# A two-layer attention and mLSTM network on one core: both value units moved behind the first pair's six projections, norm-weighted tokens on ScalarE, copies to natural order on GpSimd's queue

## The chip, the cores and the metric

The kernel runs on one core of a Trainium2 chip. The metric is the device time of one execution in microseconds (us); lower is better. Engines are named as in the profile: PE is TensorE (matmuls; PEld its weight loads), DVE is VectorE, ACT is ScalarE, POOL is GpSimd, and SP is SyncE, which issues most transfers.

## The reference

A sequence of 512 tokens of width 1024 goes through a layer of dilated attention, a feed-forward layer, an mLSTM layer and another feed-forward layer, each behind an RMS norm and with a residual, all in fp32. Only the attention layer bears on the change:

```python
def dilated_attention_mixer(xn, positions, w_in, w_out):
    proj = (xn @ w_in).reshape(B, S, N_GROUPS, 3, ATTN_HEADS, ATTN_HEAD_DIM)
    for g, (window, dilation) in enumerate(DIL_CONFIGS):          # 3 groups
        q = apply_partial_rope(proj[:, :, g, 0], positions) * scale
        k = apply_partial_rope(proj[:, :, g, 1], positions)
        v = proj[:, :, g, 2]
        o, lse = dilated_window_attention(q, k, v, window, dilation)
        ...
    wts = jax.nn.softmax(jnp.stack(lses), axis=0)
    o = jnp.einsum('gbsh,gbshd->bshd', wts.astype(xn.dtype), jnp.stack(outs))
    return o.reshape(B, S, ATTN_WIDTH) @ w_out
```

with `xn = rms_norm(x, g)`, that is x times the inverse root of its mean square per token, times a gain g per column. There are 8 heads of 128 and 3 groups, so `w_in` is 1024 x 9216.

## The kernel before, in words

**Products.** Each fp32 matrix is split into a high and a low part (`_h`, `_l`), and a product is three matmuls (high x high, high x low, low x high). Weights come in chunks of 512 KB: a load on SP's queue into one of three `wraw` buffers, then `split_chunk` (L204), in which ScalarE copies the high part (L209) and VectorE subtracts it from the chunk to get the low part (L210). There are three buffers for the high parts and three for the low ones, so the loads run a little ahead of PE. `project` (L245) makes q or k of one group for two heads: two chunks, 48 matmuls at L240 of 128x512, into two PSUM banks (suffix `_0`, `_1`), each of which VectorE evacuates (L887 or L889) and whose first 32 rows are then rotated (L521 to L527).

**Names.** `a0g1q_k0_h` is the high part of chunk 0 of the weights of attention pair 0, group 1, q. A pair is two heads; four pairs make the layer. `xa_h`, `xa_l` are the transposed tokens, already times the gain. The inverse norm (`inverse_rms`, L308) is not applied to the tokens: it is worked out beside the first projection in small instructions on 128x4 (L193, L194, L496, and others), spread over the partitions by eight diagonal matrices `xdg` (L324) and two matmuls `xbc` (L330), copied to `xrbc` (L331), and multiplied in at each evacuation.

**Order.** The program is written for the most part in the order of its work. The framework puts instructions into one queue per engine in the order in which they are written; `defer(n, f)` writes f after n more calls of `advance`, which stands after each chunk's matmuls, and `fenced` keeps other work out of a group of matmuls. An engine works through its queue strictly in order, and buffers of a pool tag (`pt`, `qk`, `v12`, `heads`, each with one or more buffers) are handed on from one tile to the next, which waits for the last reader of the one before.

**Values.** The values of group 0 (`v0`, 1024 columns) and of groups 1 and 2 (`v12`, 512 columns each, for the first two pairs) are not projected chunk by chunk. The class `Values` (L585) makes each as a 2 x 2 block product with seven block products instead of eight. This needs sums of blocks of the weights and sums of blocks of the tokens:

- The weights: `begin` (L608) loads block a11 into `first`, a21 into `own`, both on SP, and adds a22 to `own` by an accumulating transfer on GpSimd's queue (L604). `prepare` (L621) splits one chunk of the next block each time it is called, adds `first` to `own` on VectorE (L637) and adds a21 to `first` by another accumulating transfer.
- The tokens: `token_forms` (L550) scales all eight token tiles by the gain (`scaled`, L557, into `xg`), makes differences and sums of half tokens (`vz`, L567 and others) and splits four of them (T1 to T4, L538). It is written in three parts, `forms[0..2]`.
- `run` (L642) does the products in `V_ORDER`, 24 matmuls at L663 for each block product. Results of `v0` are staged in `vstage0`, `vstage1` and copied by `settle` (L693) to natural order in `v0`: 32 transfers of 64 KB, each 32x512, which may start when a stage's quarter is complete.

**The first pair before the change** goes: a0g0k and a0g0q (the first of them in an order of its own at the start of the program), then `forms[0]`, a0g1q, `forms[1]`, a0g1k, `forms[2]`, then `values_stage` (v0, then v12), then a0g2q, a0g2k. The scores of group 0 (`scores0`) are deferred by two chunks after a0g1k. While v0 runs, it calls `v12.prepare`; while v12 runs, it prefetches chunks of a0g2q.

Of the kernel before, what the change touches and what calls it, by code (L numbers as in the profile page):

```python
# [34 lines left out]
RUN_AT = (2, 2, 4, 9)  # L35
# [5 lines left out]
HALF = SEQ // 2  # L41
# [30 lines left out]
def tile_hybrid_dilated_attn_mlstm(  # L72
# [35 lines left out]
            nc.tensor.matmul(idle_ps, ones_r, idle_w, start=True, stop=True)  # L108
    idle(10)
    cols = cp.tile([P, 80], F32, name="cols")  # L110
    rows = cp.tile([80 - KC, P], F32, name="rows")
    row_of = {"attn": 0}

    def load_rows():
        r0 = KC
        for key, src in (
            ("mlstm", mlstm_norm[0:1]), ("ffn", ffn_norm), ("head", mlstm_head_gain[0:1]),
            ("convb", mlstm_conv_b[0:1]), ("convw", mlstm_conv_w[0]),
        ):
            flat = src.rearrange("a (r p) -> (a r) p", p=P)  # L120
            n = flat.shape[0]
            row_of[key] = r0
            nc.gpsimd.dma_start(rows[r0 - KC:r0 - KC + n, :], flat)
            r0 += n

    def transpose_rows():
        tp = ps.tile([P, 512], F32, tag="t", name="rowsT", bufs=1)
        nc.tensor.transpose(tp[:, :80 - KC], rows, ident[:80 - KC, :80 - KC])
        nc.vector.tensor_copy(cols[:, KC:], tp[:, :80 - KC])

    def col(key, i):
        return cols[:, row_of[key] + i:row_of[key] + i + 1]
# [7 lines left out]
    def defer(n, fn):  # L140
        later.append((tick[0] + n, next(order), fn))
# [62 lines left out]
    def split_chunk(chunk):  # L204

        raw, n, view, name = chunk
        hi = wp.tile([P, 1024], F32R, tag="whi", name=name + "_h", bufs=W_BUFS)
        lo = wp.tile([P, 1024], F32R, tag="wlo", name=name + "_l", bufs=W_BUFS)
        nc.scalar.activation(hi[:, :n], raw[:, :n], AF.Copy)  # L209
        nc.vector.tensor_tensor(lo[:, :n], raw[:, :n], hi[:, :n].bitcast(F32), op=ALU.subtract)  # L210
        return view(hi), view(lo)
# [134 lines left out]
    with ExitStack() as actx:  # L346
# [6 lines left out]
        part = lambda at, w: acst[:, at - K_MA:at - K_MA + w]  # L353
        mask_band, mask_causal, mask_dil, perm = part(K_MA, 2 * P), part(K_M1, P), part(K_M2, P), part(K_G, P)
        boot = ap.tile([P, 4, SEQ], F32, tag="v12", name="boot", bufs=2)
        cosn, sinn = boot[:R, 1], boot[:R, 2]
# [35 lines left out]
        def tok_tile(name):  # L392
            return ap.tile([P, 2, SEQ], F32, tag="qk", name=name, bufs=6)
# [12 lines left out]
        load_rows()  # L406
# [48 lines left out]

        def squares(hf):
            for tb in range(TB):
                nc.scalar.activation(boot[:, 3], xtok[:, tb, hf * 512:(hf + 1) * 512], AF.Square,
                                     accum_out=ss2[:, hf, tb:tb + 1])

        ACT, DVE = mybir.EngineType.Activation, mybir.EngineType.DVE
# [38 lines left out]
        behind(box["finish"], engine=DVE)  # L500
        for k in range(4, 8):
            x_keep(k)
        defer(5, transpose_rows)

# [45 lines left out]
        def token_forms():  # L550
            xg = ap.tile([P, KC, SEQ], F32, tag="heads", name="xg")
            lo_, hi_ = xg[:, :4], xg[:, 4:]
            z = ap.tile([P, 4, HALF], F32, tag="pt", name="vz", bufs=2)

            def scaled(ks):
                for k in ks:
                    nc.vector.tensor_scalar(xg[:, k], h[k], col("attn", k), None, op0=ALU.mult)  # L557
# [27 lines left out]
        class Values:  # L585
# [20 lines left out]
                    nc.sync.dma_start(view, self.source(key, ch))  # L606

            def begin(self):  # L608
                flat = lambda t: t.rearrange("p a s -> p (a s)")
                for key, tag in (("first", "qk"), ("own", "pt")):  # L610
                    for ch in range(2):
                        n = "%s%s%d" % (self.name, key, ch)
                        self.raw[key, ch] = (flat(tok_tile(n)) if tag == "qk" else
                                             ap.tile([P, 1024], F32, tag="pt", name=n, bufs=2))
                for ch in range(2):
                    self.load("a11", ch, self.raw["first", ch])
                for ch in range(2):
                    self.load("a21", ch, self.raw["own", ch])
                    self.load("a22", ch, self.raw["own", ch], True)
# [70 lines left out]
        def staged_values():  # L690
            stage = [ap.tile([P, TB, 512], F32, tag="v12", name="vstage%d" % i, bufs=2) for i in range(2)]

            def settle(i, c):  # L693
                for b in range(TB):
                    nc.sync.dma_start(v_all[0][32 * c:32 * c + 32, b, i * 512:(i + 1) * 512],
                                      stage[i][32 * b:32 * b + 32, c])
            return stage, settle

# [12 lines left out]
        def values_stage():  # L711
            v0_unit.prepare(2)
            v_all.append(ap.tile([P, TB, D], F32, tag="heads", name="v0"))
            v0_unit.run(v12_unit.prepare, settle)
            vq = [ap.tile([P, TB, 512], F32, tag="v12", name="vq%d" % i, bufs=2) for i in range(2)]
            v_all.append(vq[::-1])

            def g2q(n):
                ready.append(split_chunk(weight_chunk(w_in, len(ready), 6 * D, 4, "a0g2q_k%d" % len(ready))))
            v12_unit.run(g2q)  # L720

        def o_head(k):
            return v_all[0][:, :, k * P:(k + 1) * P]
# [1 line left out]
        def attention_pair(pr):  # L725
# [150 lines left out]
            for g in range(3):  # L876
# [3 lines left out]
                for part in range(2):  # L880
# [22 lines left out]
                        sh0 = sh  # L903
                    else:
                        rotate(t, sh, g == 0)
                    if pr == 0 and g == 1:
                        forms[1 + part]()
                    qk.append(t)
                if pr == 0 and g == 0:
                    forms[0]()  # L910
                if pr == 0 and g == 1:
                    values_stage()
                if g == (pr == 0):
                    defer(RUN_AT[0], lambda: run(lambda: scores0(*qks[0])))
# [757 lines left out]
```

## Time and profile before

| what | value |
|---|---|
| time, three runs | 1448.89, 1452.92, 1446.08 us, median 1448.89 |
| the profiled execution | 1448.05 us; its span 1446.2 us, mean granted clock 0.993 |
| PE busy | 1419.0 us, 98% of the span, 7968 matmuls |
| PEld busy | 1240.4 us, 86% |
| DVE busy | 991.3 us, 69% |
| ACT busy | 616.5 us, 43% |
| POOL busy | 62.7 us, 4% |
| transfers | 156.54 MB, mean 108 GB/s |

The profile is of one execution. Its span runs from the first to the last instruction and leaves out 1.85 us of what the execution's time holds around it. A row of a timeline reads: start, duration, engine, line, operation, output <- inputs, shapes and types, number of instructions joined in the row, and in brackets the idle time before it and what ended that. A row of the waits reads: who waited <- for whom, total us, how often, the longest. In rows of one engine equal instructions in a row are joined, so a row's duration can be that of several. SPq and POOLq are rows of queued transfers. Buffer numbers are left out of names, and k0 and k1 may read as `k`.

PE is busy 98% of the span, but a busy PE is not always at full pace: `PEclk` is the granted clock, and a matmul of 512 columns takes longer when it is low. So both the gaps and the slow stretches count.

### The profile page before, as it was taken

Reading aid. Unit: us, or ns where it says so; the run is one execution under the profiler, and the core shown is the slowest. Engines: PE = TensorE matmul, PEld = TensorE weight load, DVE = VectorE, ACT = ScalarE, POOL = GpSimd, SP = SyncE. Lnnn points to the kernel's source line nnn. Section 1 sums busy time; section 2 is a strip of 40 time slices with the busy share of each in tenths; the row PEclk is TensorE's granted clock in tenths of the full one; section 3 lists DMA queues with packets and bytes.
Section 4 is the critical chain, followed back from the end, with each engine's and each line's share of the span. In section 5 each row is a group of like instructions: output and inputs, shape, how many; then the busy total and the mean of one; then the engine's idle time right before and its main releaser. Section 6 shows DMA issues by size and latency. Waiting matters only on the chain. (4 is left out here: it accounts for less than half of the span.)

```text
span 1446.2 us, 20245 instructions
## 1 busy us (share of the span) xinstructions
PE 1419.0 (98%) x7968; PEld 1240.4 (86%) x7968; DVE 991.3 (69%) x1705; ACT 616.5 (43%) x1019; POOL 62.7 (4%) x99
## 2 busy tenths in 40 slices
PE   9798999999999999999999999999999999999998
PEld 7687888888888888999998888798888899998886
DVE  7865587775767487877782358987758777776233
ACT  6144432323225244444562243785534345455223
POOL 1010001010100100000000000000000000001001
PEclk9899999999999999999999999999999999999999
DMA  6465326262622534233223332221133333224231
GB/s 200 120 167 125 116 74 185 85 197 74 197 86 75 182 102 146 66 110 118 88 83 107 95 97 73 74 88 59 61 105 97 116 118 101 80 84 132 73 105 70
DMA packets 130390, 156.54 MB, mean 108 GB/s; under 512 B 6836, under 2 KB 112628, under 8 KB 130296
## 3 DMA queue, kind: packets, MB, share of 16 engines
q1 hardware_dynamic: 122928, 133.65, 29.9%
q0 software_dynamic: 5712, 20.49, 5.4%
q8 instruction: 62, 1.02, 0.3%
q10 hardware_dynamic: 1656, 1.12, 0.2%
q14 instruction: 32, 0.26, 0.1%
HBM read 143.18 MB, written 9.96 MB: 106 GB/s over the span
## 5 line engine op out<-in xcount | busy, mean ns | idle before, releaser
L1607 PE MATMUL fin<-fw_h,f1hh 128*128 128x512 f32 (+1 forms) x198 | 72.8, 368 | 0.0
L1607 PE MATMUL fin<-fw_l,f1hh 128*128 128x512 f32 (+1 forms) x198 | 72.5, 366 | 0.0
L1607 PE MATMUL fin<-fw_h,f1hl 128*128 128x512 f32 (+1 forms) x198 | 72.4, 366 | 0.0
L210 DVE TENSOR_TENSOR fw_l<-fw_w,fw_h 128x1024 fp32r<-128x1024 f32 x22 | 27.1, 1234 | 65.5 <-ACT fw_h L209 65.5
L210 DVE TENSOR_TENSOR fo_k_l<-fo_k_w,fo_k_h 128x1024 fp32r<-128x1024 f32 (+1 forms) x24 | 27.2, 1135 | 62.0 <-ACT fo_k_h L209 62.0
L240 PE MATMUL fo<-f0hh,fo_k_h 128*128 128x512 f32 x176 | 68.5, 389 | 0.0
L240 PE MATMUL fo<-f0hl,fo_k_h 128*128 128x512 f32 x176 | 68.5, 389 | 0.0
L240 PE MATMUL fo<-f0hh,fo_k_l 128*128 128x512 f32 x176 | 68.5, 389 | 0.0
L209 ACT ACTIVATE fo_k_h<-fo_k_w 128x1024 fp32r<-128x1024 f32 (+1 forms) x24 | 23.8, 990 | 74.4 <-PE fo L240 72.1
L209 ACT ACTIVATE fw_h<-fw_w 128x1024 fp32r<-128x1024 f32 x22 | 23.3, 1060 | 67.8 <-PE fin L1607 67.8
L1607 PEld LDWEIGHTS fin<-fw_l,f1hh 128*128 128x128 f32 x198 | 37.4, 189 | 6.1 <-DVE fw_l L210 0.2
L1607 PEld LDWEIGHTS fin<-fw_h,f1hl 128*128 128x128 f32 x198 | 37.3, 189 | 6.0
L1607 PEld LDWEIGHTS fin<-fw_h,f1hh 128*128 128x128 f32 x198 | 37.4, 189 | 6.0
L240 PEld LDWEIGHTS fo<-f0hh,fo_k_h 128*128 128x128 f32 x176 | 33.0, 188 | 6.9
L240 PEld LDWEIGHTS fo<-f0hl,fo_k_h 128*128 128x128 f32 x176 | 33.0, 188 | 6.8
L240 PEld LDWEIGHTS fo<-f0hh,fo_k_l 128*128 128x128 f32 x176 | 33.0, 188 | 6.8
L240 PE MATMUL f0j<-n_h,f0j_h 128*128 128x512 f32 x96 | 37.5, 390 | 0.0
L240 PE MATMUL f1j<-n_h,f1j_h 128*128 128x512 f32 x96 | 37.5, 390 | 0.0
L240 PE MATMUL f0j<-n_h,f0j_l 128*128 128x512 f32 x96 | 37.4, 389 | 0.0
L240 PE MATMUL f1j<-n_h,f1j_l 128*128 128x512 f32 x96 | 37.4, 389 | 0.0
L240 PE MATMUL f0j<-n_l,f0j_h 128*128 128x512 f32 x96 | 37.3, 389 | 0.0
L240 PE MATMUL f1j<-n_l,f1j_h 128*128 128x512 f32 x96 | 37.3, 389 | 0.0
(2132 smaller groups left out, 4892.6 us busy)
## 6 DMA issues: line engine op xcount, KB each, us to landing
f0j_w<-in_ffn_w_in_dram SPq DMA_DIRECT2D x28, 512.0 KB, 4.9
f1j_w<-in_ffn_w_in_dram SPq DMA_DIRECT2D x28, 512.0 KB, 3.6
fw_w<-in_ffn_w_out_dram SPq DMA_DIRECT2D x22, 512.0 KB, 3.8
fo_k_w<-in_ffn_w_out_dram SPq DMA_DIRECT2D x20, 512.0 KB, 3.4
awo_k_w<-in_attn_w_out_dram SPq DMA_DIRECT2D x8, 512.0 KB, 3.8
mv_k_w<-in_mlstm_w_in_dram SPq DMA_DIRECT2D x8, 512.0 KB, 3.6
mqk_k_w<-in_mlstm_w_in_dram SPq DMA_DIRECT2D x8, 512.0 KB, 3.7
mo_k_w<-in_mlstm_w_in_dram SPq DMA_DIRECT2D x8, 512.0 KB, 3.6
```

What stands on the lines that cost most here:

```text
L209: nc.scalar.activation(hi[:, :n], raw[:, :n], AF.Copy)
L210: nc.vector.tensor_tensor(lo[:, :n], raw[:, :n], hi[:, :n].bitcast(F32), op=ALU.subtract)
L240: nc.tensor.matmul(acc, whl[a][:, k, m * P:(m + 1) * P], pairs[b][kk], start=(kk == 0 and (a, b) == SPLITS[0]), stop=(kk == nk - 1 and (a, ...
L1607: nc.tensor.matmul(acc[i][:, cs], a[a_][kk][:, tb * P:(tb + 1) * P], whl[b_][:, k, cs], start=(kk == 0 and (a_, b_) == SPLITS[0]), stop=(k ...
```

## The change

Six edits, all in the attention layer's first pair or ahead of it.

1. `values_stage` stands after all six projections of pair 0 (behind a0g2k) and no longer after the first four. The three parts of the token forms stand behind a0g1k, a0g2q and a0g2k, and no longer behind a0g0q, a0g1q and a0g1k. `scores0` of group 0 is deferred by one chunk after a0g2k. Since pair 0 has no projection left, the last weights fetched while v12 runs are a1g0q's.
2. `scaled` runs on ScalarE (`activation` with a scale) and no longer on VectorE. `vz` lies in the first half of the tile `boot`; the other users of `boot` (cosines, sines, squares) move up to make room.
3. `first` and `own` of a chunk are the two halves of one tile of tag `pt` (`v0w0`, `v0w1`, `v12w0`, `v12w1`); before, `first` had tag `qk` and `own` had `pt`.
4. The 32 copies of `settle` are issued on GpSimd's queue and no longer on SP's.
5. `rows`, 72 rows of gains and biases for later layers, lies in the attention's pool (tag `ex2`) and is handed to `load_rows` and `transpose_rows`.
6. The two tiles of `v12`'s results stand in their natural order, not reversed.

```diff
-            z = ap.tile([P, 4, HALF], F32, tag="pt", name="vz", bufs=2)
+            z = boot[:, 0:2].rearrange("p a s -> p (a s)").rearrange("p (k n) -> p k n", k=4)
...
-                    nc.vector.tensor_scalar(xg[:, k], h[k], col("attn", k), None, op0=ALU.mult)
+                    nc.scalar.activation(xg[:, k], h[k], AF.Copy, scale=col("attn", k))
...
-                flat = lambda t: t.rearrange("p a s -> p (a s)")
-                for key, tag in (("first", "qk"), ("own", "pt")):
-                    for ch in range(2):
-                        n = "%s%s%d" % (self.name, key, ch)
-                        self.raw[key, ch] = (flat(tok_tile(n)) if tag == "qk" else
-                                             ap.tile([P, 1024], F32, tag="pt", name=n, bufs=2))
+                for ch in range(2):
+                    t = ap.tile([P, 2, 1024], F32, tag="pt", name="%sw%d" % (self.name, ch), bufs=2)
+                    self.raw["first", ch], self.raw["own", ch] = t[:, 0], t[:, 1]
...
-                    nc.sync.dma_start(v_all[0][32 * c:32 * c + 32, b, i * 512:(i + 1) * 512],
+                    nc.gpsimd.dma_start(v_all[0][32 * c:32 * c + 32, b, i * 512:(i + 1) * 512],
...
-            v_all.append(vq[::-1])
-
-            def g2q(n):
-                ready.append(split_chunk(weight_chunk(w_in, len(ready), 6 * D, 4, "a0g2q_k%d" % len(ready))))
-            v12_unit.run(g2q)
+            v_all.append(vq)
+
+            def following(n):
+                ready.append(split_chunk(weight_chunk(w_in, len(ready), 256, 4, "a1g0q_k%d" % len(ready))))
+            v12_unit.run(following)
...
-                    if pr == 0 and g == 1:
-                        forms[1 + part]()
                     qk.append(t)
-                if pr == 0 and g == 0:
-                    forms[0]()
-                if pr == 0 and g == 1:
+                    if pr == 0 and 3 <= 2 * g + part:
+                        forms[2 * g + part - 3]()
+                if pr == 0 and g == 2:
                     values_stage()
-                if g == (pr == 0):
-                    defer(RUN_AT[0], lambda: run(lambda: scores0(*qks[0])))
+                if g == (2 if pr == 0 else 0):
+                    defer(1 if pr == 0 else RUN_AT[0], lambda: run(lambda: scores0(*qks[0])))
```

The changed kernel's line numbers are one to five lower than those of the kernel before.

VectorE's queue around the inverse norm, before. `xr` is the norm in the making, `xg` the scaled tokens, `xrhl` its split.

```order
L193 TENSOR_TENSOR xr_a_323<-xr_a_323,xv_306 128x4
L567 TENSOR_TENSOR xg_362<-xg_362,vz_363 128x4x256
L194 SCALAR_TENSOR_TENSOR xr_320<-xr_a_323,xr_320 128x4
L572 TENSOR_TENSOR xg_362<-xg_362 128x4x256
L318 CAST xrhl_335<-xr_320 128x4
L706 TENSOR_SCALAR nrtok_354<-xr_320 128x4
L210 TENSOR_TENSOR a0g1q_k0_l_359<-a0g1q_k0_w_356,a0g1q_k0_h_358 128x1024
L319 TENSOR_TENSOR xrhl_335<-xr_320,xrhl_335 128x4
L324 TENSOR_SCALAR xdg_338<-cst_67,xrhl_335 128x128 x4
L324 TENSOR_SCALAR xdg_343<-cst_67,xrhl_335 128x128 x4
```

The same place now:

```order
L192 TENSOR_TENSOR xr_a_323<-xr_a_323,xv_306 128x4
L193 SCALAR_TENSOR_TENSOR xr_320<-xr_a_323,xr_320 128x4
L317 CAST xrhl_335<-xr_320 128x4
L703 TENSOR_SCALAR nrtok_354<-xr_320 128x4
L209 TENSOR_TENSOR a0g1q_k0_l_359<-a0g1q_k0_w_356,a0g1q_k0_h_358 128x1024
L318 TENSOR_TENSOR xrhl_335<-xr_320,xrhl_335 128x4
L323 TENSOR_SCALAR xdg_338<-cst_67,xrhl_335 128x128 x4
L323 TENSOR_SCALAR xdg_343<-cst_67,xrhl_335 128x128 x4
L209 TENSOR_TENSOR a0g1q_k1_l_475<-a0g1q_k1_w_472,a0g1q_k1_h_474 128x1024
```

The instructions on `xg` of 128x4x256 no longer stand between the small ones of the norm.

PE's queue at the first chunk of a0g1k, before:

```order
L240 MATMUL a0g1q_1_456<-xa_h3_140,a0g1q_k1_l_484 128x512
L240 MATMUL a0g1k_0_528<-xa_h0_134,a0g1k_k0_h_532 128x512
L240 MATMUL a0g1k_0_528<-xa_l0_135,a0g1k_k0_h_532 128x512
L240 MATMUL a0g1k_1_529<-xa_h0_134,a0g1k_k0_h_532 128x512
L240 MATMUL a0g1k_1_529<-xa_l0_135,a0g1k_k0_h_532 128x512
L240 MATMUL a0g1k_0_528<-xa_h0_134,a0g1k_k0_l_533 128x512
```

And now, where `rowsT` is the transpose of `rows` and a0g2q is the projection that follows:

```order
L239 MATMUL a0g1q_1_447<-xa_h3_140,a0g1q_k1_l_475 128x512
L239 MATMUL a0g1k_0_510<-xa_h0_134,a0g1k_k0_h_514 128x512
L239 MATMUL a0g1k_0_510<-xa_l0_135,a0g1k_k0_h_514 128x512
L127 MATMUL rowsT_542<-cst_67,rows_128 128x72
L239 MATMUL a0g1k_1_511<-xa_h0_134,a0g1k_k0_h_514 128x512
L239 MATMUL a0g1k_1_511<-xa_l0_135,a0g1k_k0_h_514 128x512
L239 MATMUL a0g2q_0_591<-xa_h0_134,a0g2q_k0_h_595 128x512
L239 MATMUL a0g2q_0_591<-xa_l0_135,a0g2q_k0_h_595 128x512
L239 MATMUL a0g1k_0_510<-xa_h0_134,a0g1k_k0_l_515 128x512
```

Three more instructions than before now stand ahead of the first matmul on the low part of `a0g1k_k0`: `rowsT` and two of a0g2q.

SP's queue around the copies, before:

```order
L606 DMA v12first0_874<-in_attn_w_in_dram 128x2x512
L606 DMA v12first1_875<-in_attn_w_in_dram 128x2x512
L695 DMA v0_625<-vstage0_352 32x512 x8
L695 DMA v0_625<-vstage1_353 32x512 x16
L606 DMA v12a121_w_948<-in_attn_w_in_dram 128x2x512
L606 DMA v12a220_w_1114<-in_attn_w_in_dram 128x2x512
```

The same copies now, on GpSimd's queue:

```order
L604 DMA v0w1_747<-in_attn_w_in_dram 128x2x512
L692 DMA v0_762<-vstage0_352 32x512 x15
L692 DMA v0_762<-vstage1_353 32x512 x8
L604 DMA v12w0_1011<-in_attn_w_in_dram 128x2x512
L604 DMA v12w1_1012<-in_attn_w_in_dram 128x2x512
L692 DMA v0_762<-vstage1_353 32x512 x8
L604 DMA v12w0_1011<-in_attn_w_in_dram 128x2x512
L604 DMA v12w1_1012<-in_attn_w_in_dram 128x2x512
```

SP's queue now holds loads only. On GpSimd's queue the accumulating loads of v12 (L604) stand behind copies.

PE's matmuls are the same in number and kind, and PE's order is the same again from the first chunk of the projection a1g0k to the end.

More of the change, by code (lines that the diff above doesn't have):

```diff
@@ L110, in tile_hybrid_dilated_attn_mlstm, with load_rows @@
     cols = cp.tile([P, 80], F32, name="cols")
-    rows = cp.tile([80 - KC, P], F32, name="rows")
     row_of = {"attn": 0}
-    def load_rows():
+    def load_rows(rows):
         r0 = KC
@@ L124, in load_rows, with transpose_rows @@
             r0 += n
-    def transpose_rows():
+    def transpose_rows(rows):
         tp = ps.tile([P, 512], F32, tag="t", name="rowsT", bufs=1)
@@ L355, in tile_hybrid_dilated_attn_mlstm @@
         boot = ap.tile([P, 4, SEQ], F32, tag="v12", name="boot", bufs=2)
-        cosn, sinn = boot[:R, 1], boot[:R, 2]
+        cosn, sinn = boot[:R, 2], boot[:R, 3]
         sinr = ap.tile([R, SEQ], F32, name="sinr")
@@ L405, in tile_hybrid_dilated_attn_mlstm @@
         nc.sync.dma_start(cst[:, K_MT:], consts[:, K_MT:K_MA])
-        load_rows()
+        rows = ap.tile([80 - KC, P], F32, tag="ex2", name="rows")
+        load_rows(rows)
         pair = x_tiles("xa")
@@ L457, in squares @@
             for tb in range(TB):
-                nc.scalar.activation(boot[:, 3], xtok[:, tb, hf * 512:(hf + 1) * 512], AF.Square,
+                nc.scalar.activation(boot[:, 1], xtok[:, tb, hf * 512:(hf + 1) * 512], AF.Square,
                                      accum_out=ss2[:, hf, tb:tb + 1])
@@ L502, in tile_hybrid_dilated_attn_mlstm @@
             x_keep(k)
-        defer(5, transpose_rows)
+        defer(5, lambda: transpose_rows(rows))
         def by_block(t):
```

## The prediction

> **What bounds the kernel now.** I read the windows first, to see where TensorE is not busy or not at full clock. Columns after the window and its length: busy time of PE, PEld, DVE, ACT, POOL with counts, then granted clock, DMA share, GB/s.
>
> ```profile
> 36.00:72.00 36.00, 28.60 (x105) 22.39 (x106) 32.10 (x56) 6.30 (x7) 1.19 (x1) 0.85 0.44 121
> 108.00:145.00 37.00, 33.23 (x139) 26.45 (x138) 19.16 (x17) 18.50 (x22) 2.42 (x2) 0.95 0.52 125
> 181.00:217.00 36.00, 36.00 (x178) 30.38 (x177) 29.31 (x91) 12.35 (x40) 0.00 (x0) 1.00 0.24 74
> ```
>
> In the first two PE is idle 7.4 and 3.8 us, with its clock down to 0.85 and 0.95; in the third, when the first pair is done, neither. Next the waits of PE up to 400 us: four of 2.4 us or more, all before 127 us.
>
> ```profile
> PE v_acc L663 <- ACT v12a_h L209: 3.6, 1, 3.6
> PE v_acc L663 <- DVE v0a_l L210: 3.3, 1, 3.3
> PE a0g1q L240 <- DVE rot L521: 2.9, 1, 2.9
> PE a0g1q L240 <- DVE a0g1q_k_l L210: 2.4, 1, 2.4
> ```
>
> The timeline of PE gives what each really costs (start, duration, instruction).
>
> ```profile
> 23.31 0.39 PE L240 MATMUL a0g0k<-xa_h,a0g0k_k_h 128*128 128x512 f32 x1
> 34.19 0.39 PE L240 MATMUL a0g1q<-xa_h,a0g1q_k_h 128*128 128x512 f32 x1
> 38.27 0.63 PE L240 MATMUL a0g1q<-xa_h,a0g1q_k_l 128*128 128x512 f32 x1
> 38.70 0.63 PE L330 MATMUL xbc<-xdg,ones_r 128*128 128x512 f32 x1
> 41.15 0.40 PE L240 MATMUL a0g1q<-xa_l,a0g1q_k_h 128*128 128x512 f32 x1
> 44.37 0.23 PE L128 MATMUL rowsT<-cst,rows 72*128 72x72 f32 x1
> 51.42 0.39 PE L240 MATMUL a0g1q<-xa_l,a0g1q_k_h 128*128 128x512 f32 x1
> 65.72 0.62 PE L663 MATMUL v_acc<-v0a_h,xa_h 128*128 128x512 f32 x2
> 75.29 0.39 PE L663 MATMUL v_acc<-v0a_h,xa_h 128*128 128x512 f32 x1
> 105.29 0.47 PE L663 MATMUL v_o<-v0a_h,vT4h 128*128 128x512 f32 x1 [0.42 <-DVE vstage L650]
> 118.78 0.39 PE L663 MATMUL v_acc<-v12a_h,xa_l 128*128 128x512 f32 x1
> 126.59 0.39 PE L663 MATMUL v_acc<-v12a_h,xa_l 128*128 128x512 f32 x1
> ```
>
> From 23.31 to 34.19 there are 48 matmuls, 0.2267 each. After a stall they come every 0.43 us (38.27 to 38.70) for some microseconds: the clock is paid on top of the gap. Lost, as elapsed time less instructions times 0.2267: 34.19 to 41.15, 12 of them, 4.24; 44.37 to 51.42, 11, 4.56; 65.72 to 75.29, 15, 6.17; 118.78 to 126.59, 9, 5.77. **Sum 20.74 us**; this is all that the change can win. The gap of 0.42 at 105.29 left no slow matmuls behind it.
>
> Why each stall? The first three are VectorE's. In 36:72 it is busy 32.10 of 36 us, and it got there with a late start, since the token forms stand inside the chain of small instructions that makes the inverse norm:
>
> ```profile
> 25.82 0.16 DVE L496 TENSOR_TENSOR xv<-x_ss 128x4 f32<-128x4 f32 x1 [2.49 <-ACT boot L458]
> 35.76 0.16 DVE L318 CAST xrhl<-xr 128x4 fp32r<-128x4 f32 x1
> 37.11 1.66 DVE L324 TENSOR_SCALAR xdg<-cst,xrhl 128x128 fp32r<-128x128 f32 x8
> 40.64 0.69 DVE L331 COPY xrbc<-xbc 128x512 f32<-128x512 f32 x1 [0.75 <-PE xbc L330]
> 42.45 1.20 DVE L547 SCALAR_TENSOR_TENSOR vT<-xg,vT 128x1024 fp32r<-128x1024 f32 x1
> 43.58 0.67 DVE L887 TENSOR_TENSOR a0g_q<-a0g0q,xrbc 128x512 f32<-128x512 f32 x1
> 48.46 2.33 DVE L524 TENSOR_TENSOR rot<-rot,sinr 32x1024 f32<-32x1024 f32 x2
> 50.72 1.28 DVE L527 TENSOR_TENSOR a0g_q<-a0g_q,rot 32x512 f32<-32x512 f32 x2
> 53.13 0.67 DVE L889 TENSOR_TENSOR a0g_q<-a0g1q,xrbc 128x512 f32<-128x512 f32 x1
> ```
>
> The fourth is SP's: 24 copies to natural order held its queue, and the chunk v12a121 came behind them.
>
> ```profile
> 99.71 17.89 SPq L695 DMA_DIRECT2D v<-vstage  x24
> 117.64 14.66 SPq L606 DMA_DIRECT2D v12a_w<-in_attn_w_in_dram  x3
> ```
>
> ```profile
> 121.67 1.06 ACT L209 ACTIVATE v12a_h<-v12a_w 128x1024 fp32r<-128x1024 f32 x1 [4.54 <-DMA v12a_w<-in_attn_w_in_dram]
> ```
>
> **The change part by part.** PE's matmuls are the same in number, and PE's order is the same again from the projection a1g0k on, so the sum is the stalls that go less the stalls that come.
>
> *The inverse norm comes earlier.* Without token forms between them, thirteen dependent steps of four columns run from L496 to L318. Two such rows of a later norm show the step:
>
> ```profile
> 525.54 0.16 DVE L193 TENSOR_TENSOR n1r_a<-n1r_a,n1v 128x4 f32<-128x4 f32 x1
> 525.74 0.16 DVE L194 SCALAR_TENSOR_TENSOR n1r<-n1r_a,n1r 128x4 f32<-128x4 f32 x1
> ```
>
> 13 x 0.2 is 2.6, so L318 starts at 28.4 and not 35.76. From L318 to the end of the eight xdg it was 37.11 + 1.57 - 35.76 = 2.92 (the eight overlap what follows by some 0.09); so now 31.34. In the new order the first xbc is PE's 32nd instruction from 23.31, due at 30.34; its four xdg are there about 0.8 before 31.34. Wait 0.28. It was at 38.70. Stall 1 goes: a0g1q_k0_l stands two small instructions behind L318 and takes 1.13, so it is ready by 29.9; PE wants it at 34.9.
>
> *VectorE's way to a0g1k.* Every 1024-column instruction takes 1.13 (48.46 to 50.72, two). From 31.34: a0g1q_k1_l 1.13; three readers of xbc 1.81 (40.64 to 42.45); the difference z 1.13; evacuation and rotation of both a0g0 halves 9.55 (43.58 to 53.13, the same sixteen); two evacuations of a0g1q 2.44 (a pair L887, L521 is 1.22: 43.58 to 48.46, four); a0g1k_k0_l 1.13. End 48.53. PE reaches a0g1k, 98 instructions after 23.31 and the wait, at 45.81. Five instructions later, 46.95, it wants the bank of a0g1q_1, free at 47.40: wait 0.45. After two matmuls, 47.85, it wants a0g1k_k0_l: wait 0.68. Stall 2 was for the bank of a0g0k_0: now wanted at 39.7, evacuated at 31.34 + 1.13 + 1.81 + 1.13 + 3 x 1.22 = 39.07. Gone, with 0.6 to spare.
>
> Stall 3 was for v0a110's low part, the first of the value weights. Between a0g1k_k0_l and it VectorE now has sixteen 1024-column instructions (1.13) and four evacuations with rotation (1.22 each), 23.0 us: 48.53 + 23.0 = 71.5. PE reaches it 243 matmuls after 23.31 and the waits above: 23.31 + 55.09 + 1.41 = 79.8. Stall 3 goes, with 8 us to spare.
>
> *Scaled tokens on ScalarE.* Eight of 128x512, at the price of the nearest row, 0.6:
>
> ```profile
> 12.64 2.43 ACT L227 ACTIVATE xa_h<-xT,cols 128x512 fp32r<-128x512 f32 x4 [2.01 <-PE xT L306]
> 26.15 1.07 ACT L209 ACTIVATE a0g1q_k_h<-a0g1q_k_w 128x1024 fp32r<-128x1024 f32 x1
> ```
>
> That is 4.8 us on an engine that was busy 6.30 of the 36 us from 36 on. Three stand ahead of a0g1q_k1_h: 27.1 + 1.8 + 1.0 = 29.9, wanted by VectorE at 31.34. The fourth is done by 30.6, z wants it at 34.3. Cost nothing; with that slack of 1.4 us gone, its excess would go straight into a0g1q.
>
> *Copies on GpSimd's queue.* SP no longer holds them: v12a121 follows the release of its buffer (v0a220's split, before 102) and is landed long before ScalarE can use it. Stall 4 goes. But on POOL's queue sixteen copies of the first stage and eight of the second now stand ahead of the accumulating loads of v12's own, which v12s1 needs. Rows for both:
>
> ```profile
> 104.40 1.41 DVE L650 SCALAR_TENSOR_TENSOR vstage<-v_o,nrtok,vstage 128x512 f32<-128x512 f32 x2
> 217.10 2.25 POOL L848 DMA_DIRECT2D a0pD<-a0pB  x4 [86.75 <-DVE a0pB L845]
> v12own<-in_attn_w_in_dram POOLq DMA_DIRECT2D x2, 512.0 KB, 9.9
> DMA to landing us min/median/max: 6.9/8.3/11.4
> ```
>
> In the old times: the second stage's fold frees the copies at 105.1; eight at 0.56 end at 109.6; the first load lands 9.9 later at 119.5, split on ScalarE 1.06 and VectorE 1.13: 121.7. PE, without stall 4, wants the high part at 118.78 + 13 x 0.2267 = 121.73 and the low part 0.23 later. Just in time: 0. Bounds: landing in 6.9 leaves 3 us to spare; landing in 11.4 costs 1.3 (121.7 + 1.5 - 121.96), and copies at 0.75, as SP issued them (17.89 / 24), 1.5 more, with a slow clock behind.
>
> What else moves costs nothing: v12's loads wait for v0's weights in the same buffers, as v12first did; the scores of group 0 now stand one chunk into a1g0q, whose matmuls hide their reductions; rows, boot and the order of vq change addresses only. The wait at 105.29 and its like stay.
>
> **Sum.** 20.74 - 0.28 - 0.45 - 0.68 = 19.3. Against the profiled execution, 1448.05: 1428.7. The median of the runs is 0.84 above it, so **1429.6**.
>
> On the clock: gaps of 0.42 leave none, gaps of 2.37 do. The Trainium skill (TensorE: Matmul & The Clock Gate, Why this matters for your kernels) advises against gaps over about 3 us only; the trace differs, the two gaps of 2.4 and 2.9 halved the pace. By the page they would have cost 3.4 us less and the sum would be 15.9, an estimate; the rows decide.
>
> **The rivals.** *VectorE stays late (A).* If two 1024-column instructions more come before a0g1k_k0_l, the 0.68 becomes 2.9, and the clock drops as in stall 2 (4.56 - 2.9 = 1.7): 4.0 more, 1433.6. For: VectorE works without a pause from 25.8 to 55. Against: the sum above has every instruction.
>
> *v12's adds land late (B).* 1.3 to 2.8 of stall, and of clock what stalls 1 and 4 had, 4.24 - 2.4 = 1.8 and 5.77 - 3.6 = 2.2: 1432.7 to 1434.6. For: the copies' own transfers are in flight with it. Against: this tile's four loads had a median of 8.3, and with it nothing waits.
>
> *Early loads crowd (C).* v0's weights, 1.5 MB, are loaded right behind a0g0k, and their adds run beside a0g1q_k0, which has 1.4 us to spare. If it comes 1.5 to 3 late: 0.1 to 1.6, and 1.8 of clock, 1431.5 to 1433. For: the loads stand ahead of a0g1q's on SP's queue. Against: a0g1q_k0_h was already split at 26.15, 8 us before PE wanted it.
>
> *The stalls return (D).* The change takes only the scaled tokens off VectorE:
>
> ```profile
> 25.93 0.49 DVE L557 TENSOR_SCALAR xg<-h,cols 128x512 f32<-128x512 f32 x1
> ```
>
> Eight are 3.9 us. If its waits only move, that and stall 4 are won, or stall 4 alone: 1448.89 - 9.7 = 1439.2 to 1443.1. Against: the new order puts 44 matmuls of a0g2 between VectorE's late work and its next need.
>
> *Slower: copies starve behind VectorE (E).* If each copy's descriptors had to wait out a VectorE instruction of 1.23, it would cost 0.56 + 1.23 = 1.79; sixteen from 99.71 end at 128.4, plus 11.4 to land and 2.2 to split is 142.0, 20 us after PE wants it, and 2.2 of clock: 1451.9. It is slower by over 0.5% from 1456.1, another 4.2 / 16, so from 2.05 us a copy. The Trainium skill (SBUF — State Buffer, SBUF: two separate sides) has this trap: GpSimd cannot write descriptors while VectorE holds the shared port in a two-port mode, and it advises the SP or ACT queue. Against: the four issues at 217.10 took 0.56 each beside a busy VectorE.
>
> **How the numbers follow.** Forecast 0.60, A 0.15, B 0.10, C 0.04, D 0.07, E 0.04. A measurement of this kernel can tell about 0.5%, 7.2 us. Faster by more: the first four and 0.01 of D, 0.90; within: 0.06 of D and 0.01 of E, 0.07; slower: 0.03 of E. Range: no new stall at all, 1428.2, less 2 for the runs' spread, 1426; A and B together, 1429.6 + 4.0 + 5.0, 1438.6, so 1439. It leaves out D and E, 0.11, and what I don't see.
>
> **What would show it.** Right: xbc near 30.5 us, no PE wait over 1 us before 127, granted clock 1.0 from 36 to 145, the projection a1g0k begun about 19 us earlier than before. A shows as a wait for a0g1k_k_l over 2 us; B as ScalarE waiting for v12w's DMA before v12s; C as a wait for xdg over 1 us; E as POOL issues of over 1 us. Wrong altogether if PE's lost time before a1g0k stays above 12 us.

## The result, and the profile after

The changed kernel takes 1437.79 us (median of five runs, 1434.03 to 1440.11) against 1448.89 before: a ratio of 0.9922, 95% interval 0.9892 to 0.9951. That is 11.1 us faster where 19.3 were forecast. The profiled execution took 1437.79 with a span of 1435.7; its forecast was 1428.7, so 9.1 us are missing.

The windows come first again (columns as before). The stretch from 36 to 72 is at full clock and nearly gapless; the one from 108 to 145 is not.

```profile
36.00:72.00 36.00, 35.20 (x155) 28.49 (x154) 35.60 (x54) 9.58 (x10) 0.00 (x0) 1.00 0.40 102
108.00:145.00 37.00, 33.77 (x140) 26.89 (x139) 20.59 (x20) 17.42 (x21) 16.75 (x28) 0.95 0.87 192
```

The waits of PE in the first 400 us: all four old stalls are gone. The small waits are the forecast ones; the two for `v12s` are the chunk of v12's third product.

```profile
PE v_s L660 <- ACT v12s_h L208: 2.0, 1, 2.0
PE v_s L660 <- DVE v12s_l L209: 0.8, 1, 0.8
PE a0g2q L239 <- DVE rot L521: 0.5, 1, 0.5
PE a0g1k L239 <- DVE a0g1k_k_l L209: 0.3, 1, 0.3
PE xbc L329 <- DVE xdg L323: 0.3, 1, 0.3
```

On PE's timeline that stall is seen to cost more than its 2.8 us of gaps: matmuls behind it come in twos of 1.05 and not of 0.62.

```profile
129.93 0.39 PE L660 MATMUL v_acc<-v12a_h,xa_l 128*128 128x512 f32 x1
132.37 0.49 PE L660 MATMUL v_s<-v12s_h,vT 128*128 128x512 f32 x1 [2.05 <-ACT v12s_h L208]
133.63 0.80 PE L660 MATMUL v_s<-v12s_l,vT 128*128 128x512 f32 x1 [0.77 <-DVE v12s_l L209]
134.22 1.05 PE L660 MATMUL v_s<-v12s_h,vT 128*128 128x512 f32 x2
140.57 0.39 PE L660 MATMUL v_o<-v12s_h,vT 128*128 128x512 f32 x1
180.57 0.48 PE L239 MATMUL a1g0k<-xa_h,a1g0k_k_h 128*128 128x512 f32 x1
```

From 129.93 to 140.57 stand 25 matmuls: 10.64 - 25 x 0.2267 = **5.0 us lost**. The projection a1g0k, from which on the order is the old one, starts 14.2 us earlier than its old 194.79; 194.79 - 19.3 = 175.5 was forecast, and 180.57 is 5.1 later.

Why v12s came late is on GpSimd's queue and in one row of ScalarE:

```profile
108.40 3.91 POOL L692 DMA_DIRECT2D v<-vstage  x8 [10.53 <-DVE vstage L647]
117.42 4.03 POOL L692 DMA_DIRECT2D v<-vstage  x8 [5.11 <-DMA v<-vstage]
125.08 2.48 POOL L604 DMA_DIRECT2D v12w<-in_attn_w_in_dram  x2 [3.63 <-DMA v<-vstage]
```

```profile
131.26 1.06 ACT L208 ACTIVATE v12s_h<-v12w 128x1024 fp32r<-128x1024 f32 x1 [5.70 <-DMA v12w<-in_attn_w_in_dram]
```

Eight copies go out at 0.49 each, and then GpSimd waits for a *landing* of a copy, not for data: 5.11 us before the next eight, 3.63 more before v12's accumulating loads. The loads are issued at 125.08, land about 6.2 later, and PE has been waiting since 130.3.

The other 4.0 us are behind a1g0k. One half-clock stretch in the mLSTM layer costs 1.5: from the first matmul of mqk to the first of mo it is 90.8 us in this execution and 89.3 to 89.4 before and in all other profiles (its row is in the last section). From a1g0k to the issue of the last store it is still only 1.1 us longer than before (1248.3 for 1247.2), since 0.4 comes back elsewhere, and 0.2 more than before stands outside the span (1437.79 - 1435.7 for 1.85). The rest, 2.6, is at the very end. The last row of ScalarE is the issue of the last store; the span's end is in the page's first line. Before, and after:

```profile
1442.03 0.34 ACTq L1645 DMA_DIRECT2D out_dram<-ht  x1
...
span 1446.2 us, 20245 instructions
```

```profile
1428.88 0.34 ACTq L1640 DMA_DIRECT2D out_dram<-ht  x1
...
span 1435.7 us, 20230 instructions
```

From that issue to the end it was 4.2 us and is 6.8. No term of the prediction held this.

### The profile page after: what moved, and what is told of

Its sections match the earlier page's. It is cut to its first block, busy times and chain, and to the rows that moved or that the text cites. A ratio compares the mean times of both kernels' runs of the same rounds, so it can differ in the third digit from the quotient of the medians.

```text
span 1435.7 us, 20230 instructions
## 1 busy us (share of the span) xinstructions
PE 1414.7 (99%) x7968; PEld 1238.2 (86%) x7968; DVE 989.1 (69%) x1697; ACT 621.6 (43%) x1027; POOL 78.7 (5%) x131
```

## The experiments

Two things had to be explained. For the wait at v12s the **queue theory** says: of GpSimd's transfers only eight are under way at a time, and the accumulating loads stand behind sixteen copies. The **bandwidth theory** says: the loads are late because the transfer engines are 87% busy from 108 to 145 (the share in the window's row), wherever the loads stand. And the longer end had to be traced to an edit.

### The changed kernel again

> The changed kernel once more, beside the other kernels of this group. Queue theory (the 5.0 us that the change did not win are lost at v12's third product: its accumulating loads stand behind copies on GpSimd's queue, of whose transfers only eight are under way at a time) and its rival, the bandwidth theory (the loads are late because the DMA engines are full then), both expect 1434 to 1440 us and the same wait of PE for v12s_h, 1.5 to 2.5 us.

1434.38 us (1432.76 to 1435.57), ratio 0.9908, interval 0.9895 to 0.9922. The waits for v12s were 0.2, 0.8 and 0.2 this time, the loads were issued at 123.19, and the clock stayed full behind them: a1g0k at 177.36. So the loss at v12s differs from execution to execution by some 3 us (5.1 and 1.9 by the start of a1g0k), and the smaller wait was outside both expectations. The end was 6.8 us again.

### v12's accumulating loads ahead of eight copies

```diff
+            held = []
+
+            def settle_later(i, c):
+                held.append((i, c)) if i == 1 and c >= 2 else settle(i, c)
+
+            def prepare_first(n):
+                v12_unit.prepare(n)
+                while held:
+                    settle(*held.pop(0))
-            v0_unit.run(v12_unit.prepare, settle)
+            v0_unit.run(prepare_first, settle_later)
```

> The eight copies of the second stage's first half are issued behind v12's two accumulating loads instead of ahead of them; nothing else changes. Queue theory: the loads are issued by about 118 instead of 125.08, land by 125, PE's waits for v12s_h and v12s_l (2.05 and 0.77) go, the slow clock behind them goes, and the projection a1g0k starts 5.0 us earlier, at 175.6: 1432.8 us. A new wait could come where v12's results take over the second stage's buffer (up to 3 us). Bandwidth theory: the loads land no earlier than 129, the wait stays over 1 us, and the time is within 1.5 us of the changed kernel's.

1432.12 us, ratio 0.9895 (0.9880 to 0.9910). On GpSimd's queue, on ScalarE and on PE:

```profile
116.87 1.26 POOL L604 DMA_DIRECT2D v12w<-in_attn_w_in_dram  x1 [4.28 <-DMA v<-vstage]
119.95 1.19 POOL L604 DMA_DIRECT2D v12w<-in_attn_w_in_dram  x1 [1.81 <-DMA v12w<-in_attn_w_in_dram]
```

```profile
125.75 1.05 ACT L208 ACTIVATE v12s_h<-v12w 128x1024 fp32r<-128x1024 f32 x1
```

```profile
175.91 0.48 PE L239 MATMUL a1g0k<-xa_h,a1g0k_k_h 128*128 128x512 f32 x1
```

The loads go out 8 us earlier, ScalarE finds the chunk ready (no bracket: it waited for nothing), PE waits for nothing at v12s, and a1g0k starts at 175.91, 0.3 from the expected 175.6. The queue theory holds: the place on the queue decides. Bandwidth has a part all the same, since it sets how long a copy takes to land. The first eight copies here and in the changed kernel went out while the transfer engines were full (a busy share of 1.03 from 108.4 to 121.5 in the changed kernel) and landed after some 8.5 us. Eight issues take 3.9 us, so whoever comes ninth waits. The gain in time is 2.3 us against the kernel run beside it, whose own wait was small that time.

### Each copy in two halves

```diff
                 for b in range(TB):
+                    for s in range(2):
-                    nc.gpsimd.dma_start(v_all[0][32 * c:32 * c + 32, b, i * 512:(i + 1) * 512],
-                                      stage[i][32 * b:32 * b + 32, c])
+                        nc.gpsimd.dma_start(v_all[0][32 * c:32 * c + 32, b, i * 512 + s * 256:i * 512 + (s + 1) * 256],
+                                            stage[i][32 * b:32 * b + 32, c, s * 256:(s + 1) * 256])
```

> The changed kernel with each copy cut into two of half the size: 64 transfers of 32 KB, the same bytes. Queue theory (eight of GpSimd's transfers under way at a time, so that a copy costs its landing time over eight, whatever its size): 32 copies stand between 108 and v12's accumulating loads, four rounds of 5 to 8 us, the loads are issued at 128 to 140 instead of 123 to 125, PE waits 5 to 15 us for v12s_h: 1438 to 1449. Bandwidth theory (bytes decide): the same wait as in the changed kernel, 1434 to 1438.

1443.41 us, ratio 0.9967 (0.9955 to 0.9979). The same bytes in twice as many transfers cost 9.0 us against the changed kernel's second measurement, 2.6 of them at the end.

```profile
108.12 3.91 POOL L693 DMA_DIRECT2D v<-vstage  x8 [5.05 <-DVE vstage L647]
114.97 3.90 POOL L693 DMA_DIRECT2D v<-vstage  x8 [2.94 <-DMA v<-vstage]
...
128.34 2.52 POOL L604 DMA_DIRECT2D v12w<-in_attn_w_in_dram  x2
```

```profile
PE v_s L660 <- ACT v12s_h L208: 5.6, 1, 5.6
```

Again eight, then a wait for a landing. The loads are issued at 128.34 and the wait is 5.6: at the lower end of what the queue theory gave, since half copies land sooner (114.97 and not 117.42 for the next eight), and more than the bandwidth theory allows. But the premise that a copy costs its landing over eight, whatever its size, does not hold: of the 20.2 us from 108.12 to 128.34, 15.6 are the issue of 32 copies at 0.49 and 4.6 are waiting, where sixteen whole copies took 7.9 of issue and 8.7 of waiting. The queue pays for each issue, and for landings only as far as the issue of eight does not cover them. The end grew too: the last store is issued at 1432.19, the span ends at 1441.6, 9.4 us later.

### The copies back on SP's queue

```diff
-                    nc.gpsimd.dma_start(v_all[0][32 * c:32 * c + 32, b, i * 512:(i + 1) * 512],
+                    nc.sync.dma_start(v_all[0][32 * c:32 * c + 32, b, i * 512:(i + 1) * 512],
```

> The changed kernel with the copies back on SP's queue: all of the change but that edit. If SP's queue was the cause of the fourth stall: sixteen copies from 108.4 on at 0.75 hold back the loads of v12w1 and the copies after them v12a121, PE waits 8 to 10 us around 122 to 132, the waits at v12s are covered by that, and the time is 1443 to 1448. If the queue does not matter and only bandwidth does: within 2 us of the changed kernel's.

1435.21 us, ratio 0.9915 (0.9901 to 0.9929): 0.8 us slower than the changed kernel beside it, where 5 to 14 were expected. By the time alone the rival's 2 us would be met. The rows show the queue at work all the same, so the fourth edit, whose stall was put at 5.8 us, is worth almost nothing as made. SP's queue, PE's wait and the last store:

```profile
107.81 11.91 SPq L692 DMA_DIRECT2D v<-vstage  x16
120.31 0.88 SPq L606 DMA_DIRECT2D v12w<-in_attn_w_in_dram  x2
```

```profile
PE v_acc L660 <- ACT v12a_h L208: 3.6, 1, 3.6
```

```profile
1428.25 0.34 ACTq L1640 DMA_DIRECT2D out_dram<-ht  x1
```

A stall by SP's queue is there, as long as in the kernel before (3.6, a1g0k at 181.31), though for another chunk: the loads of v12w stand behind sixteen copies. The estimate of 8 to 10 was too long, since these loads landed some 4 us after their issue (ScalarE split the chunk at 124.33). But the end is 4.2 us (the span is 1432.4). On GpSimd's queue the copies save this stall, pay another at v12s, and pay 2.6 us at the end.

### The copies alone on GpSimd's queue

The kernel before with the same one line changed the other way (`nc.sync` to `nc.gpsimd`).

> The kernel before with only the copies moved to GpSimd's queue. There, first and own are separate tiles, own comes free earlier, and in the order on GpSimd's queue both accumulating loads of v12's own stand ahead of 24 of the 32 copies. Queue theory: the fourth stall goes (5.8 us) and no wait for v12s comes in its place, so a1g0k starts at 189.0 instead of 194.8; if the longer end of the program (2.6 us from the last matmul to the end of the span, seen in all four kernels that have the copies on GpSimd's queue and in neither of the two that have them on SP's) belongs to this edit, it comes too: 3.2 us faster than before in all, 5.8 if it does not. Bandwidth theory (the loads are late whatever their place): PE still waits over 1 us for v12's chunks, and the time is within 1 us of before.

1443.83 us against 1448.59, ratio 0.9965 (0.9953 to 0.9977): 4.8 us faster, and between the two numbers expected. The fourth stall goes and no wait for v12s comes, since here the loads go first:

```profile
96.72 2.50 POOL L604 DMA_DIRECT2D v12own<-in_attn_w_in_dram  x2 [9.82 <-DVE v0s_l L210]
98.76 3.46 POOL L695 DMA_DIRECT2D v<-vstage  x6
```

Behind the loads sixteen copies in a row went out from 110.95 to 118.76 without a wait, 0.49 each: the transfer engines' busy share was down to 0.59 there, and these copies landed in 2.1 us at the median. The end is 7.2 us (last store's issue 1433.94, span 1441.1). The projection a1g0k started at 186.37, 2.6 earlier than expected; this execution had two half-clock stretches of 3.4 us where the kernel before had five, so its time says less about the fourth stall than its rows do.

So the copies on GpSimd's queue do not bring the new wait by themselves; it takes another edit of the change with them. That this is the joint tile of `first` and `own`, which comes free later, is read from the two orders on GpSimd's queue and was not tried by itself.

### The scaled tokens back on VectorE

```diff
-                    nc.scalar.activation(xg[:, k], h[k], AF.Copy, scale=col("attn", k))
+                    nc.vector.tensor_scalar(xg[:, k], h[k], col("attn", k), None, op0=ALU.mult)
```

> The changed kernel with the scaled tokens back on VectorE. In its order all token forms stand inside the inverse norm again. If moving the scaled tokens is what frees the norm: xbc comes at about 38 instead of 30.9, PE waits about 2.4 us for a0g1q_k0_l and again for a bank of a0g0, stalls 1 and 2 are back (about 8 us with the clock), stall 3 stays away: 1444 to 1448. Rival (the later place of the value units is what removes these stalls, ScalarE only saves VectorE 3.9 us): no wait over 1 us before 60, 1437 to 1440.

1443.68 us, ratio 0.9970 (0.9956 to 0.9984): 9.3 us slower than the changed kernel beside it. Its twelve runs spread from 1440.63 to 1447.19, and the profiled one is the slowest. The norm's end on VectorE, and PE's waits:

```profile
36.81 1.23 DVE L572 TENSOR_TENSOR xg<-xg 128x1024 f32<-128x1024 f32 x1
37.95 0.16 DVE L317 CAST xrhl<-xr 128x4 fp32r<-128x4 f32 x1
```

```profile
PE a0g1q L239 <- DVE a0g1q_k_l L209: 4.9, 1, 4.9
PE a0g1q L239 <- DVE rot L521: 3.0, 1, 3.0
```

The token forms stand inside the norm, L317 comes at 37.95, and stalls 1 and 2 are back, though the code calls the forms late. So a queue does not hold instructions simply in the order in which they are written, as the paragraph on the order has it: the framework moved the forms forward to where their input is ready. That VectorE has 3.9 us less to do is less than half of what frees the norm, which ends 9.4 later here than in the changed kernel. The rest are the forms' other instructions, and in the changed kernel they can't stand there, because their input comes too late: ScalarE makes the first three scaled tiles from 27.24 and the fourth only from 31.43 on, when L317 is past (28.55). The rival is refuted; stall 3 stayed away.

### The scaled tokens alone on ScalarE

The kernel before with that line changed the other way.

> The kernel before with only the scaled tokens moved to ScalarE. The norm comes early (xbc at 30.9 instead of 38.7), but without the later place of the value units VectorE has the token forms and the first evacuations ahead of a0g1q_k1_l, which is ready at about 46.4 where PE wants it at 40.8: stalls 1 and 2 (8.8 us) become one of about 5.6 and 2 of clock, stall 3 shrinks to nothing, stall 4 stays: 5 to 8 us faster than before, 1440 to 1443. Rival (this edit alone frees VectorE enough): no wait over 1 us before 75, 15 us faster, 1433.

1445.67 us against 1448.59, ratio 0.9983 (0.9974 to 0.9991): 2.9 us faster, less than the 5 to 8 expected, and far from the rival. The two long waits before 75 us:

```profile
46.06 0.50 PE L240 MATMUL a0g1q<-xa_h,a0g1q_k_l 128*128 128x512 f32 x1 [3.01 <-DVE a0g1q_k_l L210]
64.33 0.93 PE L663 MATMUL v_acc<-v0a_h,xa_h 128*128 128x512 f32 x2 [3.01 <-ACT v0a_h L209]
```

The first is the expected one, with 3.0 and not 5.6. The second is stall 3 with another releaser: VectorE is ahead now, and the first chunk of the value weights itself is late (ScalarE waited 2.92 for its load). In the changed kernel, where the value units stand later, this wait is gone; whether the later place alone covers the load or the joint tile of the third edit helps was not separated. But the second edit does not remove the first three stalls without the others, nor the others without it.

### Forty idle instructions on GpSimd

```diff
                 if pr == 0 and g == 2:
                     values_stage()
+                    pad = cp.tile([1, 1], F32, name="pad")
+                    for _ in range(40):
+                        nc.gpsimd.memset(pad, 0.0)
```

It stands on the kernel with the loads ahead of eight copies.

> The kernel with v12's accumulating loads ahead of the second stage's copies, and 40 instructions on GpSimd that write one element each, behind the value units, where GpSimd is idle. They do nothing for the result. Theory of the long end: the 2.6 us at the end hang on one late fetch of 8 KB of instructions for GpSimd, which depends on where its program crosses a block; with 40 more instructions the crossing lies before the end, and the time from the start of fin to the end of the span is 131.7 again instead of 134.3, so 1429.5 instead of 1432.1. Rival (the long end comes with the copies on GpSimd's queue as such, or by chance): 134.3 and 1432.1.

1432.14 us against 1432.12: no change, and the end stays at 6.8 (1422.87 to 1429.7). The theory came from one fetch of instructions that stands behind the last store in the profiles with 32 copies on GpSimd's queue. Here it is gone and the long end is not, and with 64 copies the end is longer still without it. That theory fails. What the ends have in common is the number of transfers on GpSimd's queue beyond the old ones: 4.2 with none, 6.8 to 7.2 with 32, 9.4 with 64.

### The copies on SP's queue, held back until v12's loads are out

```diff
-                    nc.gpsimd.dma_start(v_all[0][32 * c:32 * c + 32, b, i * 512:(i + 1) * 512],
+                    nc.sync.dma_start(v_all[0][32 * c:32 * c + 32, b, i * 512:(i + 1) * 512],
...
+            held = []
+
+            def settle_later(i, c):
+                held.append((i, c)) if c >= 2 else settle(i, c)
+
+            def prepare_first(n):
+                v12_unit.prepare(n)
+                if len(v12_unit.todo) == 12:
+                    for ch in range(2):
+                        v12_unit.fetch("a12", ch)
+                    while held:
+                        settle(*held.pop(0))
-            v0_unit.run(v12_unit.prepare, settle)
+            v0_unit.run(prepare_first, settle_later)
```

`fetch` is the load of an a12 chunk, taken out of `prepare`.

> The changed kernel with the copies on SP's queue, but 24 of them held back until all six loads that v12 needs first have been issued; GpSimd's queue holds the accumulating loads alone. Queue theory: no wait over 0.5 us between 110 and 145, a1g0k at 175.5. Theory of the long end (from the last store's issue to the end of the span it is 4.2 us without copies on GpSimd's queue, 6.8 with 32, 9.4 with 64: 0.08 us for each): 4.2 us, and so 1429.5, against 1432.1 with the loads first on GpSimd's queue. If the end does not hang on the copies: 1432. If the copies on SP hold up a load after all: a wait of PE before 145 and 1434.

**1429.13 us** (1427.93 to 1430.44), ratio 0.9864 (0.9848 to 0.9880): the fastest kernel of the study, 20.3 us below the kernel before beside it. SP's queue, PE and the last store:

```profile
109.14 0.37 SPq L606 DMA_DIRECT2D v12a_w<-in_attn_w_in_dram  x1
109.56 18.32 SPq L698 DMA_DIRECT2D v<-vstage  x24
```

```profile
174.60 0.48 PE L239 MATMUL a1g0k<-xa_h,a1g0k_k_h 128*128 128x512 f32 x1
```

```profile
1421.94 0.34 ACTq L1658 DMA_DIRECT2D out_dram<-ht  x1
```

The last early load goes out just ahead of the 24 copies, nothing later is wanted for 18 us, and the end is 4.2 (the span is 1426.1). Counted from the first matmul of a0g0k (22.46 here, 23.31 before), a1g0k starts after 152.1 us, where the prediction had 152.2. So this kernel, with its copies on SP's queue, does what the prediction expected of the changed one.

### The same, with 32 small transfers more on GpSimd's queue

```diff
+                    for _ in range(32):
+                        nc.gpsimd.dma_start(attn_rows, attn_norm.rearrange("a (r p) -> (a r) p", p=P))
```

> The same kernel with 32 more transfers on GpSimd's queue that do nothing for the result: the attention's gain of 4 KB is loaded again over itself, long before the end. Theory of the long end, by the number of transfers on GpSimd's queue: 6.8 us from the last store's issue to the end of the span, 2.6 slower than without them, 1432.1. By their bytes or packets (4 KB instead of 64): under 0.7 us slower, 1429.5 to 1430.2.

1434.31 us, ratio 0.9900 (0.9883 to 0.9917), 5.2 slower where 2.6 or 0.7 were expected. The surplus is a side effect: the added transfers, each of which waited for the one before to land, also held up v0's accumulating loads on that queue, and PE waited 1.3 and 0.8 us in v0 (a1g0k at 177.81). The last store:

```profile
1424.48 0.34 ACTq L1660 DMA_DIRECT2D out_dram<-ht  x1
```

With a span of 1431.3 the end is 6.8 us, with transfers of 4 KB as with copies of 64. The longer end goes by the number of transfers on GpSimd's queue, 2.6 / 32 = 0.08 us each, and not by bytes. What the chip does in that time the traces do not show.

## Why the prediction was right in sign and short in size

- **The inverse norm earlier: right.** In the changed kernel VectorE has

```profile
28.55 0.17 DVE L317 CAST xrhl<-xr 128x4 fp32r<-128x4 f32 x1
```

  L317 comes at 28.55 where 28.4 was worked out, and PE's wait for xdg is 0.3 where 0.28 was. It is the second edit's doing alone: PE's wait for xdg is 0.3 in the kernel with nothing but that edit, too.
- **VectorE's way to a0g1k: right.** Waits of 0.50 and 0.30 where 0.45 and 0.68 stood in the sum. Those are idle gaps alone; with the slower matmuls around them the way from a0g0k to the value units (23.45 to 80.34, 243 matmuls) lost 1.8 us where 1.4 stood. Stalls 1 and 2 are gone, and rival A did not come. The second edit alone would not have done it: with nothing else changed, a0g1q_k1_l comes 3.0 late.
- **Stall 3: right that it goes, not why it was there.** VectorE made the low part of the first value weights from 71.38 to 72.57 (ready at 71.5 was forecast), PE reached the value units at 80.34 (79.8 forecast) and did not wait. But the prediction counted stall 3 among VectorE's. In the kernel before, the load of that chunk was late as well:

```profile
64.43 1.06 ACT L209 ACTIVATE v0a_h<-v0first 128x1024 fp32r<-128x1024 f32 x1 [3.01 <-DMA v0first<-in_attn_w_in_dram]
```

  And with VectorE ahead, in the kernel with the scaled tokens alone on ScalarE, 3.0 of it stayed. The change covers both causes, so this error did not touch the time; that was luck.
- **Scaled tokens on ScalarE at nothing: right** as a cost; as a gain the sum held them only inside the norm. Taken back to VectorE, they cost 9.3 us.
- **Copies on GpSimd's queue at nothing: this step failed.** The sentence was that the loads come "Just in time: 0", from copies "at 0.56" each. The issue is that cheap, 0.49. But eight at most are under way, and the first eight took 9 us (108.40 to 117.42) until the next could follow, so these waited 5.11 and the loads 3.63. Counted from the first of these copies (99.71 before), the loads were to go out 9.9 us later, at 109.6, and went out 16.7 later. That is 6.8 too late, of which a landing shorter than taken (6.2 for 9.9) gave back 3.7: luck, without which the stall would have been longer still. Rival B, with a chance of 0.10, named this place and its sign, ScalarE waiting for v12w's DMA, with a price of 3.1 to 5.0; it cost 5.1 and 1.9 in the two profiles. No row of the trace of before had the price. SP's 24 copies at 0.75 look like it, but SP's waits for landings were small there:

```profile
SPq L695 <- DMA v<-vstage: 1.2, 3, 0.4
```

  The rest of the 17.89 is the issue of the copies itself, 0.7 each, slower than the 0.49 on GpSimd's queue.
- **The end: not seen.** 2.6 us at the end of the program for 32 transfers on GpSimd's queue had no row in the trace of before and no term in the sum.

In the first profile: 5.1 at v12s, 1.1 from a1g0k to the last store (1.5 of clock in the mLSTM layer less 0.4 elsewhere), 2.6 at the end and 0.2 outside the span, 9.0 of the missing 9.1. In the second: 177.36 - 175.5 = 1.9 at v12s and 2.6 at the end, 4.5 of 1433.45 - 1428.7 = 4.7. With both causes taken away the kernel runs in 1429.1, 0.5 from the forecast 1429.6.

## What to carry to other kernels

Where many small transfers move to another queue, what counts is the issue of each, how many of that queue may be under way, how long each takes to land, and then who stands behind them: order the transfer that someone waits for ahead of the ones that nobody waits for, and PE waits on neither queue. An operation moved off a busy engine can be worth more through the order that its late result forces than through the time it took. And look at the stretch from the last store to the end of the span: it is part of the time.

## What the runs showed of the hardware that was not expected

- About 0.08 us more at the end of the program for each transfer added on GpSimd's queue (2.6 to 3.0 for 32 of 64 KB, 2.6 for 32 of 4 KB, 5.2 for 64 of 32 KB), though the last of them had landed over 1 ms before.
- Of GpSimd's transfers eight at most are under way in this program: the rows of 8 copies, and of 2 loads and 6 copies, each end in a wait for a landing.
- The clock falls to exactly half, for about 3.4 us at a time. In the changed kernel's profile, behind the wait at v12s and once in the mLSTM layer (the column before the last two is the clock):

```profile
133.60:137.00 3.40, 3.37 (x8) 2.69 (x9) 2.98 (x3) 2.88 (x4) 1.75 (x2) 0.50 0.42 84
915.30:918.70 3.40, 3.30 (x10) 2.82 (x11) 2.91 (x8) 1.34 (x5) 0.00 (x0) 0.50 0.00 0
```

  The Trainium skill (TensorE: Matmul & The Clock Gate, What's actually happening) gives a free-running window of about 3.4 us and two states, full and half; both rows agree.
- Where a gap lies decides whether it costs clock. With the scaled tokens alone on ScalarE, PE had two gaps of 3.01 us (their rows stand in that section). Cut time into stretches of 3.41 us, counted back from 64.69, where the half clock begins. The first gap falls into two stretches and leaves the clock full; the second falls into one, and half clock follows:

```profile
40.80:44.21 3.41, 2.26 (x10) 1.50 (x8) 3.41 (x6) 1.06 (x1) 0.00 (x0) 1.00 0.00 0
44.21:47.62 3.41, 1.56 (x7) 1.30 (x8) 3.41 (x5) 0.00 (x0) 0.00 (x0) 1.00 0.16 22
61.28:64.69 3.41, 0.40 (x3) 0.30 (x2) 2.92 (x5) 1.18 (x2) 0.00 (x0) 1.00 0.69 263
64.69:68.10 3.41, 3.08 (x8) 2.03 (x7) 3.41 (x4) 1.88 (x2) 0.00 (x0) 0.50 0.00 0
```

  Cut like that up to 1400 us in all twelve profiles, every stretch with 1.98 us or more of idle PE was followed by half clock. Of those at full clock, none with 1.51 us or less was; of four in between, two were (1.58 and 1.67) and two were not (1.81 and 1.85). So the clock in a stall's price is partly luck: stall 1, a gap of 2.32 with the copies alone on GpSimd's queue, left the clock full there, where the 2.37 before halved it. The half-clock stretch in the mLSTM layer is luck of the same kind: gaps of 1.04 and 0.75 us stand ahead of it, and 1.06 and 0.75 stand at the same place in the changed kernel's second profile and cost no clock.
